# A hybrid decoder layer on one core: k projections evicted by ScalarE, queued sums between down products, and a new order of loads

## The chip, the cores and the metric

The kernel runs on 1 core of one Trainium2 chip. TensorE (PE) multiplies into PSUM; VectorE (DVE), ScalarE (ACT) and GpSimd (POOL) work beside it; SyncE (SP) issues nearly all DMAs. Each engine takes its instructions strictly in the order of its own queue. The metric is the device time of one launch in microseconds (us), the median of several runs.

## The reference

One decoder layer on a sequence of 1024 tokens of width 1024, in float32:

```python
hn = rmsnorm(x, attn_norm_w)
da_q, da_k, da_v, ml_qk, ml_v, ml_o, ml_i, ml_f = split_projection(hn @ w_in)
da_out = diff_attention(da_q, da_k, da_v, lam, slopes)      # 4 heads, causal, ALiBi
qk = silu(causal_dwconv(ml_qk, mlstm_conv_w, mlstm_conv_b)) # width 4
mq, mk = split(qk)                                          # mLSTM queries and keys
ml_out = sigmoid(ml_o) * rmsnorm(mlstm_chunkwise(mq, mk * d**-0.5, ml_v, i_pre, logf))
x = x + concat(da_out, ml_out) @ w_out
u = causal_dwconv(rmsnorm(x, ffn_norm_w) @ w_up, ffn_conv_w, ffn_conv_b)  # D_FF 2816
gate, up = split(u)
x = x + (silu(gate) * up) @ w_down
return rmsnorm(x, final_norm_w)
```

## The kernel before

**Products.** Every float32 operand is split into a high and a low part (`split`, lines 109 to 116: ACT writes the high part on line 112, DVE or POOL subtracts on line 113), and one product is three matmuls of 128x128 by 128x512 (`mm3`, lines 155 to 157; `mm3b`, lines 160 to 162). Split weights lie in eight `w` tiles in rotation; raw weights land in two `wf` tiles.

**Start.** The projections that feed the mLSTM's convolution come first, as columns: `ct` 0 to 3 are q, `ct` 4 to 7 are k, each in two halves `hf` of 512 tokens. q halves are copied out of PSUM by ACT (lines 350, 355) and scaled in SBUF with the row `RB` of inverse norms (line 363, 128x1024). For k the loop of lines 364 to 376 takes the banks `sa`/`sb`, `mm` and `big` in turn, and DVE takes each half out of PSUM and scales it in one instruction (line 369, 128x512). The same loop stores and begins POOL's sums of rows of `w_down` (`store_sums`, `down_sums`: lines 311 to 325; POOL on line 319, DMAs on lines 316 and 325), loads and splits `wo`, the weights of the o projection (line 375, four pieces), and runs the convolution of a q column (`conv_qk`: ACT line 339, three DVE instructions on line 341, ACT's Silu on line 342). The gate matmuls follow (line 384, first on bank `sb`, then on `sa`; DVE copies them out on line 385), the convolutions of the k columns, and the o projections (`o_unit`, on `wo`), two of which stand before the gates' transposes (line 429).

**Down projection.** It is a Strassen-like scheme of seven block products, in the order p = 1, 2, 7, 5, 6, 4, 3 (`PORDER`), each of 11 steps, 77 in all; a step is 12 matmuls, three for each of four row tiles `tt`. `steps` counts them through as k. `dprep_to(k + 1 + DLEAD)` prepares step k+4: the weight load for every second step (`wload`, line 1060), sums of activations for p = 2, 7, 6, 4 (line 1103), and two splits. `fill(k)` issues the larger loads at given steps: activations (`load`, line 1042) and the residual `x2` (lines 1081, 1090). Products alternate between two sets of banks; the last product takes up the `big` banks that p = 6 wrote. At a product's end `evac` adds its four PSUM banks into the outputs on DVE (line 1144): 4 adds after p = 1, 2, 4, 3, 8 after p = 5, 20 after p = 6; `half1` (ACT line 1164, DVE line 1172) follows p = 2 and 6, `finish` follows p = 4 and the last product.

**Order.** The order on each queue is not the order of the lines. A planner places instructions as it holds them to be ready; between instructions that are ready at once the earlier line goes first. The order is fixed when the kernel is built.

Of the kernel before, what the change touches and what calls it, by code (L numbers as in the profile page):

```python
# [13 lines left out]
AF = mybir.ActivationFunctionType  # L14
ALU = mybir.AluOpType
# [5 lines left out]
NT = S // P  # L21
# [18 lines left out]
def tile_hybrid(ctx: ExitStack, tc: tile.TileContext, I: dict, out: bass.AP):  # L40
    nc = tc.nc
    V = nc.vector
    A = nc.scalar
# [22 lines left out]
    def sm8(n=8, name="s8"):  # L66
        return sp.tile([P, n], F32, name=name, tag=name)
# [37 lines left out]
    x2d = dp.tile([NT, P, D], F32, name="x2d")  # L105
# [15 lines left out]
    HV = (slice(0, 512), slice(512, 1024))  # L121
# [21 lines left out]
    def getw(ahead):  # L143
        n = used[0]
        used[0] += 1
        while len(made) < min(n + 1 + ahead, len(specs)):
            made.append(wpiece(*specs[len(made)]))
        return made[n]
# [34 lines left out]
    def rotate(n):  # L183
        return (mmps, lambda: big([P, 512]), lambda: small([P, 512]))[n % 3]()
# [57 lines left out]
    def col_piece(ct):  # L242
        cw[ct, 0], cw[ct, 1] = wpiece(I["w_st"][ct], None, V)
# [38 lines left out]
    RB = pr0.t([P, S], tag="RB")  # L282
# [19 lines left out]
    M = [pq.t([P, S], tag="mqk", bufs=8) for _ in range(8)]  # L302
# [6 lines left out]
    pairs = list(range(NJ // 2))  # L309
# [12 lines left out]
    def store_sums(n=1):  # L322
        for i, g, u in (dsum.pop(0) for _ in range(min(n, len(dsum)))):
            for k, f in enumerate((g, u)):
                nc.sync.dma_start(wsum[i, k], f)
# [4 lines left out]
    def col_mm(ps, ct, kc, hf):  # L330
        k = slice(kc % 4 * P, (kc % 4 + 1) * P)
        w = cw[ct, kc // 4]
        mm3(ps, w[:, 0, k], w[:, 1, k], *xpart(kc, hf), kc == 0, kc == KC - 1)
# [30 lines left out]
    for ct in range(4, 8):  # L364
        for hf in range(2):
            ps = rotate(2 * ct + hf)
            for kc in range(KC):
                col_mm(ps, ct, kc, hf)
            V.tensor_tensor(M[ct][:, HV[hf]], ps, RB[:, HV[hf]], op=ALU.mult)
        store_sums()  # L370
        down_sums()
        if ct == 4:
            col_piece(7)
        elif ct == 6:
            wo = [getw(0) for _ in range(4)]
        conv_qk(ct - 4)
# [367 lines left out]
    x2 = []  # L744
# [323 lines left out]

    def fill(k):

        if k == 1:
            load(a21[:, 0:4, :], "A21", (0, 4))
        elif k == 3:
            load(a12, "A12", (4, NP - 1))
        elif k == 5:
            load(a21[:, 4:8, :], "A21", (4, 8))
        elif k == 7:
            load(a21[:, 8:, :], "A21", (8, NP))
        elif k in (6, 8, 9, 10):
            tt = (6, 8, 9, 10).index(k)  # L1080
            nc.sync.dma_start(x2[tt], x2d[tt])
        elif k == 11:
            load(a12[:, NP - 5:, :], "A12", (NP - 1, NP))
        elif k == 13:
            load(a22[:, 0:6, :], "A22", (0, 6))
        elif k == 17:
            load(a22[:, 6:, :], "A22", (6, NP))
        elif k in (20, 22, 24, 26):
            tt = 4 + (k - 20) // 2
            nc.sync.dma_start(x2[tt], x2d[tt])  # L1090
        elif k == 19:
            nc.sync.dma_start(fin, I["final_norm"].partition_broadcast(P))
            V.tensor_scalar(fin, fin, RSC, None, op0=ALU.mult)
# [40 lines left out]
    x2 = [pd.t([P, D], tag="x2", bufs=8) for _ in range(NT)]  # L1134
# [8 lines left out]
    def add(dst, x, y=None):  # L1143
        V.tensor_tensor(dst, dst if y is None else x, x if y is None else y, op=ALU.add)

    def evac(p, tt, ps):
        h0, h1 = HV
        c11, c12, c21, c22 = x2[tt][:, h0], x2[tt][:, h1], x2[tt + 4][:, h0], x2[tt + 4][:, h1]
        if p in (1, 7):
            A.activation(acc[p, tt], ps, AF.Copy)  # L1150
        if p == 6:
            a1, a7 = acc[1, tt], acc[7, tt]
            add(a1, ps)
            add(a7, a1)
            add(c22, a7)
            add(c21, a7)
            add(c12, a1)
        for dst in {1: [c11], 2: [c11], 5: [c12, c22], 4: [c21], 3: [c12]}.get(p, ()):
            add(dst, ps)

    def half(tt, h, part):

        j = pd.t([P, 512], tag="junk")
        A.activation(j, x2[tt][:, HV[h]], AF.Square, accum_out=part)
# [3 lines left out]
    def half1(tt, h):  # L1168

        half(tt, h, part1[:, tt:tt + 1])  # L1170
        xx = x2[tt][:, HV[h]]
        V.tensor_tensor(xx, xx, fin[:, HV[h]], op=ALU.mult)

    def finish(tts, h):

        n = len(tts)
        c = slice(tts[0], tts[0] + n)
        v = sm8(n, f"vx{n}")
        V.tensor_scalar(v, part1[:, c], 1.0 / D, EPS, op0=ALU.mult, op1=ALU.add)
        for tt in tts:  # L1180
            half(tt, h, part2[:, tt:tt + 1])
        V.scalar_tensor_tensor(v, part2[:, c], 1.0 / D, v, op0=ALU.mult, op1=ALU.add)
        if n == 1:
            r = newton(v)
        else:
            r = rsqrt(v, n, "x")
            V.tensor_scalar(r, r, 1.0 / RSC, None, op0=ALU.mult)
        a_, b_ = HV[1 - h], HV[h]
        for i, tt in enumerate(tts):
            xx, ri = x2[tt], r[:, i:i + 1]  # L1190
            A.activation(xx[:, a_], xx[:, a_], AF.Copy, scale=ri)
            V.scalar_tensor_tensor(xx[:, b_], xx[:, b_], ri, fin[:, b_], op0=ALU.mult, op1=ALU.mult)
            if tt == 3:
                A.dma_start(out[tt, :, a_], xx[:, a_])
                nc.sync.dma_start(out[tt, :, b_], xx[:, b_])
            else:
                nc.sync.dma_start(out[tt], xx)

    k = 0
    TAIL = 5  # L1200
    for n, p in enumerate(PORDER):
        ps = banks(n)
        last = n == len(PORDER) - 1
        for i in range(NP - TAIL if last else NP):
            dprep_to(k + 1 + DLEAD)
            fill(k)
            for tt in range(4):
                dmm(ps[tt], k, tt, i == 0, i == NP - 1)
            k += 1
        if not last:  # L1210
            for tt in range(4):
                evac(p, tt, ps[tt])
            if p == 2:
                for tt in range(4):
                    half1(tt, 0)
            elif p == 6:
                for tt in range(4, NT):
                    half1(tt, 1)
            elif p == 4:
                finish(range(4, NT), 0)  # L1220
        else:
            dprep_to(len(steps))
            for tts in LAST:
                for tt in tts:
                    for i in range(TAIL):
                        dmm(ps[tt], k + i, tt, False, i == TAIL - 1)
                    evac(p, tt, ps[tt])
                finish(tts, 1)
    psA.close()
    pd.close()  # L1230
# [64 lines left out]
```

## Time and profile before

| | us |
|---|---|
| median of 3 runs | 1242.09 (1241.46 to 1242.48) |
| profiled execution, its time | 1244.75 |
| profiled execution, its span | 1242.8 |
| PE busy | 1195.4 (96%) |
| DVE busy | 906.0 (73%) |
| ACT busy | 568.0 (46%) |
| POOL busy | 479.5 (39%) |
| DMA, mean over the span | 123 GB/s |

The profiled execution lies 2.66 us above the median and has 1.95 us outside its span. Times in rows are us from the start of the span. PE is busy nearly throughout, so the rows to look at are the few in which it waits, and what came last there.

### The profile page before, as it was taken

What the parts mean: (1) busy time and instruction counts of PE and PEld (TensorE: products, weight loads), DVE (VectorE), ACT (ScalarE), POOL (GpSimd) and SP (SyncE); (2) the same over time, 40 slices, a digit from 0 to 9 for tenths busy, and PEclk for the clock granted to TensorE, in tenths of its full rate; (3) what the DMA queues carried; (4) which work ended last, traced back from release to release, by engine and by line L of the source; (5) the groups of instructions that cost most, each with busy time, mean ns of one, the idle gap of its engine ahead of it and who ended that gap; (6) DMA issues with size and microseconds to landing.
All of it is one profiled execution on the core that took longest, in us unless ns stands there. A gap on an engine that the chain in (4) does not pass through costs nothing.

```text
span 1242.8 us, 15880 instructions
## 1 busy us (share of the span) xinstructions
PE 1195.4 (96%) x5600; PEld 973.8 (78%) x5600; DVE 906.0 (73%) x1568; ACT 568.0 (46%) x1106; POOL 479.5 (39%) x364
## 2 busy tenths in 40 slices
PE   7996999999999999999899999999999999999996
PEld 6884877888778878888688888888888887888775
DVE  5589232566667777679998878788787786986774
ACT  6533223333666665444543444434434344544443
POOL 0474410003443431001788888787787600000000
PEclk9997999999999999999999999999999999999999
DMA  8756442214212252333122222212212169623223
GB/s 310 234 215 243 163 170 78 76 68 156 74 51 52 68 167 97 119 111 111 46 91 102 85 99 71 85 68 85 100 71 85 51 212 380 244 96 98 73 94 135
DMA packets 60015, 153.26 MB, mean 123 GB/s; under 512 B 5984, under 2 KB 10272, under 8 KB 59936
## 3 DMA queue, kind: packets, MB, share of 16 engines
q1 hardware_dynamic: 59648, 151.47, 35.9%
q8 instruction: 44, 0.72, 0.2%
q10 hardware_dynamic: 288, 0.79, 0.2%
q14 instruction: 35, 0.29, 0.1%
HBM read 112.35 MB, written 35.68 MB: 119 GB/s over the span
## 4 chain that ended last, share of the span: by engine, by line
PE 80%; DVE 7%; DMA 4%; ACT 3%; POOL 2%; issue 2%; SPq 1%; ACTq 0%; POOLq 0%; DVEq 0%
PE mm L157 6%; PE mm L155 6%; PE mm L156 6%; PE mm L160 4%; PE mm L161 4%; PE mm L162 4%; PE big L157 4%; PE big L155 4%; PE big L156 4%; PE big L160 3%; PE big L161 3%; PE big L162 3%; PE sb L724 3%; POOL vda L319 2%; PE sa L157 2%; PE sa L155 2%
## 5 line engine op out<-in xcount | busy, mean ns | idle before, releaser
L112 ACT ACTIVATE w<-wf 128x512 fp32r<-128x512 f32 x162 | 99.0, 624 | 136.6 <-POOL w L113 25.4
L113 DVE TENSOR_TENSOR w<-wf,w 128x512 fp32r<-128x512 f32 x130 | 110.8, 861 | 38.1 <-ACT w L112 33.5
L981 DVE SCALAR_TENSOR_TENSOR y<-x2b,fcw,y 128x1022 f32<-128x1022 f32 x44 | 88.7, 2056 | 0.0
L980 DVE SCALAR_TENSOR_TENSOR y<-x2b,fcw,y 128x1023 f32<-128x1023 f32 x44 | 74.2, 1726 | 10.3 <-ACT y L979 10.3
L113 POOL TENSOR_TENSOR w<-s,w 128x512 fp32r<-128x512 f32 x40 | 69.3, 1733 | 6.5 <-ACT w L112 6.5
L113 POOL TENSOR_TENSOR w<-wu,w 128x512 fp32r<-128x512 f32 x40 | 67.5, 1687 | 2.1 <-ACT w L112 2.1
L113 POOL TENSOR_TENSOR w<-wf,w 128x512 fp32r<-128x512 f32 x32 | 45.3, 1418 | 59.5 <-ACT w L112 47.0
L319 POOL TENSOR_TENSOR vda<-vda 128x512 f32<-128x512 f32 x24 | 42.7, 1794 | 65.0 <-DMA vda<-in_w_down_dram 64.2
L155 PE MATMUL mm<-xb,w 128*128 128x512 f32 x168 | 66.8, 397 | 0.0
L156 PE MATMUL mm<-xb,w 128*128 128x512 f32 x168 | 66.4, 395 | 0.0
L157 PE MATMUL mm<-xb,w 128*128 128x512 f32 x168 | 66.4, 395 | 0.0
L699 DVE CUSTOM_DVE_ANT_0 s<-big,B 128x128 f32<-128x128 f32 (+7 forms) x64 | 47.6, 755 | 14.4 <-PE big L697 12.8
L979 ACT ACTIVATE y<-x2b,fcw 128x1024 f32<-128x1024 f32 x44 | 52.3, 1236 | 10.5 <-DVE x2b L970 9.1
L160 PE MATMUL big<-w 128*128 128x512 f32 x132 | 52.4, 398 | 3.8 <-ACT w L112 3.0
L915 POOL TENSOR_TENSOR s<-wu 128x512 f32<-128x512 f32 x22 | 38.4, 1745 | 43.9 <-DMA wu<-in_w_up_dram 43.9
L701 ACT ACTIVATE s<-s,mb 128x128 f32<-128x128 f32 (+7 forms) x64 | 49.3, 772 | 11.7 <-DVE mb L700 10.6
L161 PE MATMUL big<-w 128*128 128x512 f32 x132 | 51.9, 393 | 0.0
L162 PE MATMUL big<-w 128*128 128x512 f32 x132 | 51.5, 391 | 0.0
L112 ACT ACTIVATE w<-s 128x512 fp32r<-128x512 f32 x45 | 28.3, 629 | 50.5 <-PE mm L157 16.1
L916 POOL TENSOR_TENSOR s<-s,wf 128x512 f32<-128x512 f32 x22 | 42.5, 1933 | 20.0 <-DMA wf<-in_w_up_dram 18.2
L112 ACT ACTIVATE w<-hb 128x512 fp32r<-128x512 f32 x41 | 25.7, 628 | 51.8 <-PE big L162 24.2
L724 PEld LDWEIGHTS sb<-vda,aT 128*128 128x128 f32 x288 | 36.2, 190 | 15.3 <-ACT aT L721 14.5
(507 smaller groups left out, 3787.1 us busy)
## 6 DMA issues: line engine op xcount, KB each, us to landing
wf<-in_w_up_dram SPq DMA_DIRECT2D x22, 512.0 KB, 4.5
wu<-in_w_up_dram SPq DMA_DIRECT2D x22, 512.0 KB, 3.4
actd<-y SPq DMA_DIRECT2D x21, 512.0 KB, 2.6
wf<-in_w_st_dram SPq DMA_DIRECT2D x12, 512.0 KB, 4.0
vda<-in_w_down_dram SPq DMA_DIRECT2D x12, 512.0 KB, 6.4
wsum<-vda SPq DMA_DIRECT2D x12, 512.0 KB, 2.8
wf<-in_w_mv_dram SPq DMA_DIRECT2D x12, 512.0 KB, 4.6
wf<-wsum SPq DMA_DIRECT2D x12, 512.0 KB, 3.4
```

The costliest lines, as they stand in the source:

```text
L112: A.activation(dst[:, 0, :], src, AF.Copy)
L113: loeng.tensor_tensor(dst[:, 1, :], src, dst[:, 0, :].bitcast(F32), op=ALU.subtract)
L155: PE.matmul(ps, sh, mh, start=first, stop=False)
L156: PE.matmul(ps, sh, ml, start=False, stop=False)
L157: PE.matmul(ps, sl, mh, start=False, stop=last)
L160: PE.matmul(ps, sh, w[:, 0, :], start=first, stop=False)
L161: PE.matmul(ps, sl, w[:, 0, :], start=False, stop=False)
L162: PE.matmul(ps, sh, w[:, 1, :], start=False, stop=last)
L319: GP.tensor_tensor(dst, x_, y, op=ALU.subtract)
L724: PE.matmul(ops, aT[:, b * P:(b + 1) * P], vda[k // 2][:, k % 2, h * P:(h + 1) * P], start=k == 0, stop=k == qt)
L980: V.scalar_tensor_tensor(y[:, 1:], u[:, :S - 1], cw[:, 1:2], y[:, 1:], op0=ALU.mult, op1=ALU.add)
L981: V.scalar_tensor_tensor(y[:, 2:], u[:, :S - 2], cw[:, 0:1], y[:, 2:], op0=ALU.mult, op1=ALU.add)
```

## The change

Three parts. (1) In the loop over the k columns ACT copies each half out of PSUM, and one DVE instruction for each column then scales it in SBUF. (2) In the down projection the adds after a product, and the `half1` and `finish` that follow, go into a list `later`; each step of the next product issues three entries of it behind its preparation. In the last product the adds of a group of row tiles are issued together behind the group's matmuls. (3) In `fill` the activation loads move: A21's first part from step 1 to 2, A12's from 3 to 4, A21's second from 5 to 6, A21's third from 7 to 12, A12's last from 11 to 12; the four x2 loads go from steps 6, 8, 9, 10 to 8, 9, 10, 11.

```diff
@@ -366,7 +366,8 @@
             ps = rotate(2 * ct + hf)
             for kc in range(KC):
                 col_mm(ps, ct, kc, hf)
-            V.tensor_tensor(M[ct][:, HV[hf]], ps, RB[:, HV[hf]], op=ALU.mult)
+            A.activation(M[ct][:, HV[hf]], ps, AF.Copy)
+        V.tensor_tensor(M[ct], M[ct], RB, op=ALU.mult)
         store_sums()
         down_sums()
@@ -1068,18 +1069,16 @@
     def fill(k):
-        if k == 1:
+        if k == 2:
             load(a21[:, 0:4, :], "A21", (0, 4))
-        elif k == 3:
+        elif k == 4:
             load(a12, "A12", (4, NP - 1))
-        elif k == 5:
+        elif k == 6:
             load(a21[:, 4:8, :], "A21", (4, 8))
-        elif k == 7:
+        elif k in (8, 9, 10, 11):
+            nc.sync.dma_start(x2[k - 8], x2d[k - 8])
+        elif k == 12:
             load(a21[:, 8:, :], "A21", (8, NP))
-        elif k in (6, 8, 9, 10):
-            tt = (6, 8, 9, 10).index(k)
-            nc.sync.dma_start(x2[tt], x2d[tt])
-        elif k == 11:
             load(a12[:, NP - 5:, :], "A12", (NP - 1, NP))
@@ -1143,20 +1142,25 @@
+    later = []
+    def work(n):
+        for _ in range(min(n, len(later))):
+            later.pop(0)()
     def evac(p, tt, ps):
...
         if p == 6:
             a1, a7 = acc[1, tt], acc[7, tt]
-            add(a1, ps)
-            add(a7, a1)
-            add(c22, a7)
-            add(c21, a7)
-            add(c12, a1)
-        for dst in {1: [c11], 2: [c11], 5: [c12, c22], 4: [c21], 3: [c12]}.get(p, ()):
-            add(dst, ps)
+            pairs = [(a1, ps), (a7, a1), (c22, a7), (c21, a7), (c12, a1)]
+        else:
+            pairs = [(dst, ps) for dst in {1: [c11], 2: [c11], 5: [c12, c22], 4: [c21], 3: [c12]}.get(p, ())]
+        later.extend(lambda d=d, x=x: add(d, x) for d, x in pairs)
@@ -1204,6 +1208,7 @@
             dprep_to(k + 1 + DLEAD)
             fill(k)
+            work(3)
             for tt in range(4):
                 dmm(ps[tt], k, tt, i == 0, i == NP - 1)
@@ -1211,13 +1216,11 @@
             if p == 2:
-                for tt in range(4):
-                    half1(tt, 0)
+                later.extend(lambda tt=tt: half1(tt, 0) for tt in range(4))
             elif p == 6:
-                for tt in range(4, NT):
-                    half1(tt, 1)
+                later.extend(lambda tt=tt: half1(tt, 1) for tt in range(4, NT))
             elif p == 4:
-                finish(range(4, NT), 0)
+                later.append(lambda: finish(range(4, NT), 0))
@@ -1225,6 +1228,7 @@
                     for i in range(TAIL):
                         dmm(ps[tt], k + i, tt, False, i == TAIL - 1)
                     evac(p, tt, ps[tt])
+                work(len(later))
                 finish(tts, 1)
```

## Rows read from the trace of the kernel before

**Rows 1.** The waits of PE over the whole span, longest in total first: engine, bank and line that waited, what ended the wait, us in total, times, longest.

```profile
PE sa L384 <- DVE mqk L369: 10.1, 1, 10.1
...
PE big L160 <- ACT w L112: 3.0, 1, 3.0
PE mm L161 <- DVE w L113: 2.6, 1, 2.6
...
PE big L160 <- DVE x L1144: 0.8, 1, 0.8
```

**Rows 2.** The timeline of PE from 97 to 130 us: start, us, engine, line, operation and tiles, and in brackets the idle time before and what ended it.

```profile
97.74 3.87 PE L384 MATMUL sb<-xb,wg 128*16 128x512 f32 x16
111.74 6.45 PE L384 MATMUL sa<-xb,wg 128*16 128x512 f32 x16 [10.12 <-DVE mqk L369]
...
129.00 0.67 PE L429 MATMUL sb<-cst,gs 16*128 16x16 f32 x8
```

**Rows 3.** The timeline of DVE over the same stretch, its order being its queue's.

```profile
103.21 0.68 DVE L369 TENSOR_TENSOR mqk<-big,RB 128x512 f32<-128x512 f32 x1
...
105.28 5.80 DVE L341 SCALAR_TENSOR_TENSOR ta<-mqk,par,ta 128x1021 f32<-128x1021 f32 x3
111.00 0.68 DVE L369 TENSOR_TENSOR mqk<-sa,RB 128x512 f32<-128x512 f32 x1
111.60 1.27 DVE L341 SCALAR_TENSOR_TENSOR ta<-mqk,par,ta 128x1021 f32<-128x1021 f32 x1
...
115.78 1.55 DVE L113 TENSOR_TENSOR w<-wf,w 128x512 fp32r<-128x512 f32 x1
...
123.94 0.67 DVE L385 COPY gs<-sa 16x512 f32<-16x512 f32 x1
```

**Rows 4.** The timeline of ACT: an earlier copy out of PSUM (line 355), and its queue from 103 to 115 us.

```profile
53.19 0.60 ACT L355 ACTIVATE mqk<-sb 128x512 f32<-128x512 f32 x1 [3.91 <-PE sb L157]
...
103.98 1.24 ACT L339 ACTIVATE ta<-mqk,par 128x1024 f32<-128x1024 f32 x1 [2.23 <-DVE mqk L369]
107.65 1.06 ACT L342 ACTIVATE mqk<-ta 128x1024 f32<-128x1024 f32 x1 [2.43 <-DVE ta L341]
112.97 1.06 ACT L342 ACTIVATE mqk<-ta 128x1024 f32<-128x1024 f32 x1 [4.26 <-DVE ta L341]
113.93 1.13 ACT L112 ACTIVATE w<-wf 128x512 fp32r<-128x512 f32 x2
```

**Rows 5.** The instructions of lines 369 and 363: count, durations in ns (least, median, most), first and last start, shapes.

```profile
L369 DVE TENSOR_TENSOR mqk<-mm,RB x3: 675/677/682, 73.2 to 115.2; 128x512 f32<-128x512 f32 x3
...
L363 DVE TENSOR_TENSOR mqk<-mqk,RB x4: 1216/1768/2318, 55.2 to 59.7; 128x1024 f32<-128x1024 f32 x4
```

**Rows 6.** The timeline of PE where steps 5, 6 and 7 of the down projection begin.

```profile
1026.92 0.39 PE L160 MATMUL big<-w 128*128 128x512 f32 x1
...
1032.78 0.79 PE L160 MATMUL big<-w 128*128 128x512 f32 x1 [2.97 <-ACT w L112]
...
1036.96 0.40 PE L160 MATMUL big<-w 128*128 128x512 f32 x1
```

**Rows 7.** The timeline of ACT at the split of step 6's weights (tile `bw`).

```profile
1032.10 0.63 ACT L112 ACTIVATE w<-bw 128x512 fp32r<-128x512 f32 x1 [3.82 <-DMA bw<-in_w_down_dram]
```

**Rows 8.** The timeline of SP's queue at the beginning of the loads into the tiles of the down projection (line 1042: activations; line 1060: weights).

```profile
1024.78 0.37 SPq L1042 DMA_DIRECT2D a<-actd  x1
1025.24 0.46 SPq L1060 DMA_DIRECT2D bw<-in_w_down_dram  x1
1025.75 1.75 SPq L1042 DMA_DIRECT2D a<-actd  x2
```

**Rows 9.** DMA issues of four stretches, one row each: tiles, queue, count, KB each, median us from issue to landing. In order, those issued at 1024.78, 1025.24 and 1025.75 us, and those issued from 1009 to 1016 us.

```profile
a<-actd SPq DMA_DIRECT2D x1, 1024.0 KB, 5.9
...
bw<-in_w_down_dram SPq DMA_DIRECT2D x1, 512.0 KB, 6.8
...
a<-actd SPq DMA_DIRECT2D x1, 1536.0 KB, 10.4
...
wf<-in_w_down_dram SPq DMA_DIRECT2D x2, 512.0 KB, 5.6
```

**Rows 10.** The timeline of DVE at the end of product 6: the first of its 20 adds (line 1144), the four instructions of line 1172 behind the last, and the next split.

```profile
1166.89 1.28 DVE L1144 TENSOR_TENSOR acc<-acc,big 128x512 f32<-128x512 f32 x2
...
1178.92 2.48 DVE L1172 TENSOR_TENSOR x<-x,fin 128x512 f32<-128x512 f32 x4
1181.33 0.68 DVE L113 TENSOR_TENSOR w<-a,w 128x512 fp32r<-128x512 f32 x1
```

**Rows 11.** The timeline of PE at the same place: step 59 begins, waits, and step 60 begins.

```profile
1178.42 0.62 PE L160 MATMUL mm<-w,w 128*128 128x512 f32 x2
...
1182.06 0.97 PE L161 MATMUL mm<-w,w 128*128 128x512 f32 x2 [2.58 <-DVE w L113]
...
1185.39 0.59 PE L160 MATMUL mm<-w 128*128 128x512 f32 x1
```

**Rows 12.** Stretches: from and to, length, busy us (and instructions) of PE, its weight loads, DVE, ACT and POOL, then the granted clock of PE (1.00 is 2.4 GHz), the DMA share and GB/s.

```profile
110.00:120.00 10.00, 8.26 (x25) 3.92 (x26) 8.26 (x8) 3.34 (x4) 4.34 (x3) 0.63 0.87 290
...
1029.70:1042.40 12.70, 9.73 (x37) 7.84 (x37) 9.72 (x16) 4.38 (x8) 0.00 (x0) 0.87 1.05 394
...
1179.00:1186.00 7.00, 4.42 (x13) 3.17 (x12) 7.00 (x12) 1.62 (x5) 0.00 (x0) 0.76 0.13 32
```

## The prediction

> **What bounds the kernel now.** I read the page's busy shares first: PE is busy 96% of the span, so a change gains only where PE waits or runs at its lower clock. The second view is the waits of PE by line [rows 1]. Three waits belong to the parts of this change: 10.1 us at the gate matmuls (line 384) for DVE's eviction of a k half (line 369), 3.0 us for an ACT split and 2.6 us for a DVE split in the down projection. The third view is the timeline of each engine around these places, for what stands ahead of the late instruction on its queue. The reader is to see that in the first and third place DVE was not slow at the instruction that PE missed; it came to it late.
>
> A wait costs more than its length, because the clock falls with it: 0.63, 0.87 and 0.76 of 2.4 GHz in the stretches that hold the three waits [rows 12], so 1.2 GHz for part of each. So I count from where PE should have been. A down step is 2.72 us: from the beginning of step 7 (1036.96) to that of step 59 (1178.42) are 52 steps [rows 6, 11].
> - Gates: the second half was due at 97.74 + 3.87 = 101.61, began at 111.74 and took 6.45 instead of 3.87 [rows 2]. Lost: 10.1 + 2.6 = 12.7 us.
> - Step 6 was due at 1026.92 + 2.72 = 1029.64, step 7 at 1032.36; step 7 began at 1036.96 [rows 6]. Lost: 4.6 us.
> - Step 60 was due at 1178.42 + 2.72 = 1181.14 and began at 1185.39 [rows 11]. Lost: 4.25 us.
>
> **Part 1, k evictions by ACT.** It removes eight DVE instructions of 0.68 us and adds four of 128x1024, which in the same shape took 1.22 to 2.32 us [rows 5]: 5.4 us go, 4.9 to 9.3 come. DVE's work doesn't fall. ACT gets eight copies of 0.60 [rows 4], 4.8 us. What changes is who frees bank `sa`: no longer DVE, which reached the eviction at 111.00 although the bank's product had ended before 97.74.
>
> One would hope for all 12.7 us. I don't, because ACT's queue waits for DVE as well. In DVE's queue the eviction of the last column's first half stands between the second and the third convolution instruction of column 6 (the group at 105.28 is the last of column 5 and the first two of column 6; 111.60 is the third of column 6) [rows 3]. The planner held the bank to be full at that point. The copy becomes ready at the same point, but on ACT, and there it falls between the Silu of column 5 (107.65) and that of column 6 (112.97) [rows 4]. The former waits for DVE's convolution, so the copy can't pass it. How early can it start? Ahead of column 5's last convolution instruction DVE loses the two evictions of column 6, 0.6 us of queue each (one of them is the row at 103.21), and gains, ahead of it or behind it, the scaling of column 6, 1.22 to 2.32. The Silu then starts between 107.65 - 1.2 = 106.4 and 106.4 + 2.3 = 108.7 and takes 1.06; the first convolution instruction of column 6 on ACT (1.24, line 339) [rows 4] may stand between; the copy takes 0.60. PE goes on between 108.1 and 111.6, instead of 111.74; I take 109.8, the middle, for a gain of 2. The gates still run slowly, since PE has idled 8 us.
>
> What is late next: the last piece of `wo`, split by 117.3 (115.78 + 1.55) [rows 3]. The first o unit would start near 116.2 and needs it after 18 of its 24 matmuls (0.227 each, a twelfth of 2.72), at 120.3, so it is in time. Then the gates' transposes, at 129.0 now [rows 2], need DVE's copy of the gates, which ended at 124.6 [rows 3]; this caps the gain at 4.4 as long as DVE's queue ends there. Bounds of this part: 0 and 4.4; a loss is a rival below. Behind line 429 the gates' chain, the loads of the v weights and the chunks hang on PE or on each other, not on a clock of their own, so the gain is carried on.
>
> The rows of line 363 spread from 1216 to 2318 ns while POOL was summing, those of line 369 only from 675 to 682 [rows 5]. The Trainium skill (SBUF — State Buffer, Who interferes with whom) has a rule that speaks against this change: a DVE instruction with two SBUF inputs contends with a GpSimd instruction that reads SBUF, one with a single SBUF input doesn't. The trace agrees. By that rule each scaling may cost 2.32, DVE would be 3.9 us poorer, and the time would be that of the first rival.
>
> **Part 2, queued sums.** Behind product 6 DVE runs 20 adds and four instructions of line 1172 in one block from 1166.89 to 1181.33, 0.60 each, and only then the next split, for which step 59 waits [rows 10, 11]. In the changed source the preparation of step 59 stands ahead of the first three entries, and each later preparation ahead of the next three. A split that is ready then goes first. Per step of product 4 DVE has 3 x 0.6 + 2 x 0.6 = 3.0 us against PE's 2.72, so over the eight steps that empty the list (24 entries) it falls 2.3 us behind; the splits lead by three to four steps, 8 to 11 us, so PE doesn't see it. Gain: 4.25 at most; I take 4.0. Queued behind the adds are only the squares on ACT and the banks: the `big` banks of product 6 are free after 16 entries, six steps into product 4, and are wanted 11 steps after its start. After products 1, 2 and 5 PE waits for nothing now, so nothing is to be had there. In the last group PE waits 0.8 us for an add [rows 1]; that add still follows its matmuls, so I count 0.
>
> **Part 3, later loads.** The first load into the new tiles is A21's first part (1024 KB, issued 1024.78, landing after 5.9 us, at 1030.7); step 6's weights go behind it (1025.24, 6.8 us, at 1032.0); then 1536 KB of A12 (1025.75, 10.4 us, at 1036.2) [rows 8, 9]. They land one behind another, 512 KB in 1.35 us and 1536 KB in 4.1, so 0.37 MB per us. ACT's split follows at 1032.10 and PE at 1032.78 [rows 6, 7]. With A21 at step 2, `wload` of step 6 stands ahead of it and goes first, at 1024.78. It then lands as a 512 KB load does with less ahead of it, 5.6 us in the nearest row [rows 9], at 1030.4; taking off what the present first load shows (5.9 for 1024 KB, less 1.35 for the half) it is 4.5 us, at 1029.3. With 0.7 from landing to PE, step 6 starts at 1030.0 (by 5.6: 1031.1) against 1029.64 due. Gain: 4.6 - 0.4 = 4.2 at best, 1.7 if it lands after 5.6 and the slow stretch comes as before (1.45 of the 4.6); I take 4.0, since so short a wait (0.8 in rows 1) leaves the clock alone. Price on the other side: all later loads move back by 512 KB at most, 1.4 us, except A21's third part and the last of A12, which go behind the x2 loads, 2 MB or 5.5 us later. Step 11's weights come to about 1040.8 for a need at 1042; the third part of A21 to about 1051, wanted by sums of product 2 whose splits lead by four steps. Near, but covered.
>
> **Sum.** 2.0 + 4.0 + 4.0 = 10.0 us off a profiled span of 1242.8, so 1232.8 there; the runs' median lies 0.7 below that span, 1242.1, so **1232.1**. By the bounds (0 + 1.7 + 4.0 and 4.4 + 4.2 + 4.25) 1236.4 to 1229.2.
>
> **Rivals.**
> - *DVE stays the bound in the first stage.* Scalings at 2.32 us keep column 5's Silu and the copy where the eviction was: PE goes on at 111.6. For it: POOL is summing through most of this stretch. Against: two evictions fall away. Gain 8.0: 1234.1. Chance 0.21.
> - *The copy passes.* The planner puts it ahead of column 5's Silu, PE goes on at 101.6, and the next wait is for the last piece of `wo` or the gates' copies: 4.4 + 8.0, 1229.7; if DVE's queue is reordered as well so that these come early, the whole 12.7: 1221.4. Against: the Silu is ready about 2.5 us before that bank is full. Chance 0.12, a third of it for the far end.
> - *One of the down parts does not do what it says.* The planner still sets the adds in a block, since DVE looks idle to it, or A21 is still first at the door. One loss of 4.25 or 4.6 stays: 1236.2. Chance 0.09.
> - *Slower: ACT's queue takes DVE's place.* The copy falls behind column 6's Silu and the two splits of `wo` behind that. That Silu now has copy, scaling and line 339 ahead of its convolution: 112.97 plus 0.6 + 1.24 + 2 x 1.1 of collisions is 117.0; 1.06 of Silu, 1.13 of splits and 0.6 of copy give 119.8. From 119.7 on (111.74 + 8.0) this eats all that the down projection gains; with the three convolution instructions colliding too, 3 x 1.0, it is 122.8, 3.1 over: 1245.2. Against: the bank is full some 3 us before column 6's last convolution instruction. Chance 0.07.
> - The rest, 0.08, is a time near the present one: several of these bounds at once, each a little short.
>
> **How the numbers follow.** Forecast 1232.1, chance 0.43; its own range 1229 to 1236. Below 1226 lies only the far end of the second rival (0.04); above 1239 lie the slower rival and the rest (0.15). So 1226 to 1239, with 0.81 inside. A measurement of this kernel can tell about 0.2%, 2.5 us, from no change: faster (under 1239.6) 0.43 + 0.21 + 0.12 + 0.09 = 0.85, the same 0.08, slower (over 1244.6) 0.07.
>
> **What would show it.** In the profile after: line 369 as four SBUF instructions of 1.2 to 2.3 us; the wait of the gates on bank `sa` now ended by ACT, starting at 101.6 and ending between 108 and 111.6, right behind a Silu. Step 6 begins within a microsecond of step 5's end and its weights are the first load of the down tiles. Behind product 6 DVE alternates splits and threes of adds, and step 59 takes 2.72. Wrong would be: gates that go on at 101.6, or after 112; a new PE wait for line 1103 or for an x2 load around 1040 to 1055; a wait for a split in product 4.

## The result and the profile after

The changed kernel takes 1231.89 us, the median of 5 runs (1231.05 to 1236.98), beside 1242.48 for the kernel before (5 runs, 1241.46 to 1244.14): 10.6 us less. The ratio over the runs is 0.9907, 95% interval 0.988 to 0.9934; that of the two medians is 0.9915. Its profiled execution took 1232.53 with a span of 1230.7, 12.1 below the span before. Lines behind line 369 stand one further on (385 for 384, 430 for 429, 1043 for 1042, 1061 for 1060), behind `fill` one less (1143 for 1144), and behind `evac` four more (1176 for 1172). One thing has to be known to read the traces: between 650 and 990 us, where the granted clock is 1.00, matmuls follow each other at 230.2 ns in nine of the fourteen traces, 229.5 in three and 233.3 in two (4.6 us over that stretch). Each kernel has one trace, so it is not shown whether the kernel or the execution sets this; I compare stretches and not only spans.

PE's waits over the whole span, as in [rows 1]:

```profile
PE sa L385 <- ACT mqk L369: 6.6, 1, 6.6
...
PE sa L160 <- ACT w L112: 1.8, 1, 1.8
...
PE big L160 <- DVE x L1143: 0.8, 1, 0.8
...
PE sb L430 <- DVE gs L386: 0.3, 1, 0.3
```

Both waits of the down projection are gone; that of the gates went from 10.1 to 6.6 and ends with ACT. A new one stands at the v projections: 1.8 us for a split of their weights. PE's timeline beside [rows 2]:

```profile
97.64 3.87 PE L385 MATMUL sb<-xb,wg 128*16 128x512 f32 x16
108.14 5.14 PE L385 MATMUL sa<-xb,wg 128*16 128x512 f32 x16 [6.63 <-ACT mqk L369]
...
124.14 0.41 PE L430 MATMUL sb<-cst,gs 16*128 16x16 f32 x4
124.84 0.42 PE L430 MATMUL sb<-cst,gs 16*128 16x16 f32 x4 [0.29 <-DVE gs L386]
...
166.56 0.50 PE L160 MATMUL sa<-w,xb 128*128 128x512 f32 x1 [1.81 <-ACT w L112]
```

The gates go on 3.6 us earlier and run 1.3 shorter, so the transposes come 4.9 earlier; the two later waits, of 0.3 and 1.8, cost 0.4 and 2.0 of that again. Two stretches tell the rest, the first of after, the second of before (columns as in [rows 12]):

```profile
168.00:174.00 6.00, 6.00 (x21) 4.78 (x21) 0.89 (x3) 0.92 (x2) 3.48 (x3) 0.72 0.56 196
```

```profile
313.00:321.00 8.00, 7.23 (x27) 5.72 (x28) 4.94 (x21) 3.29 (x11) 4.05 (x6) 0.79 0.43 116
```

Behind the wait of 1.8 us PE's granted clock is 0.72 from 168 to 174 us, which costs another 1.6, so only 0.9 us of the lead is left. From 313 to 321 us it is the kernel before that runs slowly, behind a wait of 1.9 us for a split (line 696); after waits 1.5 there and stays at 1.00, and by 321 us its lead is 2.95. The down projection begins at 1010.50 instead of 1013.27. ACT's timeline beside [rows 4]; in brackets the idle time before:

```profile
102.65 0.63 ACT L112 ACTIVATE w<-wf 128x512 fp32r<-128x512 f32 x1 [7.25 <-DMA wf<-in_w_mv_dram]
103.19 1.04 ACT L342 ACTIVATE mqk<-ta 128x1024 f32<-128x1024 f32 x1
104.13 0.58 ACT L369 ACTIVATE mqk<-big 128x512 f32<-128x512 f32 x1
104.61 0.62 ACT L112 ACTIVATE w<-wf 128x512 fp32r<-128x512 f32 x1
105.29 1.06 ACT L342 ACTIVATE mqk<-ta 128x1024 f32<-128x1024 f32 x1
106.37 1.24 ACT L339 ACTIVATE ta<-mqk,par 128x1024 f32<-128x1024 f32 x1
107.52 0.58 ACT L369 ACTIVATE mqk<-sa 128x512 f32<-128x512 f32 x1
113.85 1.06 ACT L342 ACTIVATE mqk<-ta 128x1024 f32<-128x1024 f32 x1 [5.76 <-DVE ta L341]
114.82 1.14 ACT L112 ACTIVATE w<-wf 128x512 fp32r<-128x512 f32 x2
```

The copy out of `sa` (107.52) stands behind column 5's Silu (105.29) and line 339, as forecast. New to me is the head of the list: ACT stands idle 7.25 us for the third raw piece of `wo`, and all below it is queued behind the split of that piece. DVE's timeline, of this stretch (beside [rows 3]) and behind product 6 (beside [rows 10]):

```profile
91.23 2.31 DVE L370 TENSOR_TENSOR mqk<-mqk,RB 128x1024 f32<-128x1024 f32 x1
93.47 3.59 DVE L113 TENSOR_TENSOR w<-wf,w 128x512 fp32r<-128x512 f32 x4
96.98 4.85 DVE L341 SCALAR_TENSOR_TENSOR ta<-mqk,par,ta 128x1022 f32<-128x1022 f32 x4
103.31 0.69 DVE L113 TENSOR_TENSOR w<-wf,w 128x512 fp32r<-128x512 f32 x1 [1.48 <-ACT w L112]
103.92 1.27 DVE L341 SCALAR_TENSOR_TENSOR ta<-mqk,par,ta 128x1021 f32<-128x1021 f32 x1
...
107.94 5.82 DVE L341 SCALAR_TENSOR_TENSOR ta<-mqk,par,ta 128x1023 f32<-128x1023 f32 x3
...
124.12 0.67 DVE L386 COPY gs<-sa 16x512 f32<-16x512 f32 x1
...
1160.70 0.69 DVE L1143 TENSOR_TENSOR acc<-acc,acc 128x512 f32<-128x512 f32 x1
1161.30 0.69 DVE L113 TENSOR_TENSOR w<-a,w 128x512 fp32r<-128x512 f32 x1
1161.90 0.69 DVE L113 TENSOR_TENSOR w<-wf,w 128x512 fp32r<-128x512 f32 x1
1162.50 1.29 DVE L1143 TENSOR_TENSOR x<-x,acc 128x512 f32<-128x512 f32 x2
1163.73 0.69 DVE L113 TENSOR_TENSOR w<-a,w 128x512 fp32r<-128x512 f32 x1
```

DVE idles too for that piece (103.31). Behind product 6 it now changes between adds and splits. SP's timeline, stretch of the `wo` loads and start of the down projection (beside [rows 8]):

```profile
94.73 0.80 SPq L325 DMA_DIRECT2D wsum<-vda  x2
95.58 0.78 SPq L316 DMA_DIRECT2D vda<-in_w_down_dram  x1
96.46 1.64 SPq L126 DMA_DIRECT2D wf<-in_w_mv_dram  x2
...
1012.61 0.42 SPq L1061 DMA_DIRECT2D bw<-in_w_down_dram  x1
1022.00 0.92 SPq L1043 DMA_DIRECT2D a<-actd  x2
```

Step 6's weights (1012.61) leave 9.4 us ahead of A21's first load; before, both left together at 1024.78 and 1025.24. The windows that hold steps 6 to 10 and 58 to 60 show PE busy throughout at a granted clock of 1.00 (columns as in [rows 12]):

```profile
1026.80:1040.00 13.20, 13.20 (x59) 10.91 (x59) 9.67 (x16) 5.20 (x10) 0.00 (x0) 1.00 1.05 396
1168.00:1176.00 8.00, 8.00 (x37) 6.61 (x36) 8.00 (x15) 4.69 (x10) 0.00 (x0) 1.00 0.19 72
```

From start to start the lead over before is 2.78 us at the first down step, 7.39 at step 11, 11.65 at step 60, 11.87 at step 61 and 12.04 at the last row tile: 2.78 for part 1, 4.61 for part 3, 4.48 for part 2 and 0.17 in the last group. The last 0.2 between steps 60 and 61 are the rest of step 59's wait: before, the first matmul of step 60 still took 0.42 us and not 0.23.

### The profile page after: what moved, and what is told of

Its sections match the earlier page's. It is cut to its first block, busy times and chain, and to the rows that moved or that the text cites. A ratio compares the mean times of both kernels' runs of the same rounds, so it can differ in the third digit from the quotient of the medians.

```text
span 1230.7 us, 15875 instructions
## 1 busy us (share of the span) xinstructions
PE 1191.1 (97%) x5600; PEld 972.0 (79%) x5600; DVE 907.1 (74%) x1564; ACT 572.1 (46%) x1114; POOL 479.7 (39%) x364
## 4 chain that ended last, share of the span: by engine, by line
PE 81%; DVE 9%; DMA 4%; ACT 3%; issue 2%; POOL 0%; SPq 0%; DVEq 0%; ACTq 0%; POOLq 0%
PE mm L157 6%; PE mm L155 6%; PE mm L156 6%; PE mm L160 4%; PE big L157 4%; PE big L155 4%; PE mm L161 4%; PE big L156 4%; PE mm L162 4%; PE big L160 4%; PE big L162 4%; PE big L161 4%; PE sb L725 3%; DVE ta L341 2%; PE sa L157 2%; PE sa L155 2%
## 5 line engine op out<-in xcount | busy, mean ns | idle before, releaser
L113 DVE TENSOR_TENSOR w<-wf,w 128x512 fp32r<-128x512 f32 x130 | 108.3, 844 | 35.7 <-ACT w L112 31.2
L319 POOL TENSOR_TENSOR vda<-vda 128x512 f32<-128x512 f32 x24 | 47.4, 1991 | 62.9 <-DMA vda<-in_w_down_dram 62.2
L725 PE MATMUL sb<-vda,aT 128*128 128x128 f32 x288 | 44.2, 289 | 3.7 <-ACT aT L722 3.1
```

The source lines that it names most:

```text
L113: loeng.tensor_tensor(dst[:, 1, :], src, dst[:, 0, :].bitcast(F32), op=ALU.subtract)
L725: PE.matmul(ops, aT[:, b * P:(b + 1) * P], vda[k // 2][:, k % 2, h * P:(h + 1) * P], start=k == 0, stop=k == qt)
```

## The experiments

My theory: (A) the copy of `sa` waits in ACT's queue for what DVE and the splits of `wo` do, so bank `sa` is not itself the price; A21's first load alone cost the 4.6 us; the interleaving of adds, not the list, saves the loss at step 59. The rival for each: the bank, the other moved loads, any queue. The tables' columns are read off PE's timeline. G is the start of the first gate half; "go on" the start of the second, "transposes" that of line 429 or 430, "down" that of the first down matmul, all less G; "length" runs from there to the last down matmul; "pace" is the mean distance of matmul starts from 650 to 990 us, in ns. "Down" holds the pace too: 229.5 takes 1.0 us off it, 233.3 adds 4.6. Ratios are to the kernel before on the same chip.

| kernel | go on | transposes | down | length | pace |
|---|---|---|---|---|---|
| before | 14.00 | 31.26 | 915.53 | 219.61 | 230.2 |
| after | 10.50 | 26.50 | 912.86 | 210.33 | 230.2 |
| part 1 alone | 11.01 | 27.01 | 910.66 | 217.96 | 229.5 |
| part 2 alone | 14.75 | 32.00 | 920.39 | 213.37 | 233.3 |
| one load at step 2 | 14.54 | 30.55 | 914.48 | 214.97 | 230.2 |
| that load by POOL | 13.88 | 30.00 | 914.02 | 218.64 | 230.2 |
| without part 1 | 14.09 | 30.22 | 919.78 | 210.32 | 233.3 |
| all sums at once | 11.22 | 28.61 | 912.37 | 211.69 | 230.2 |
| gates on `big` | 3.71 | 28.42 | 910.19 | 210.30 | 229.5 |
| late sums | 10.34 | 27.73 | 911.12 | 210.34 | 230.2 |
| both of these | 3.70 | 28.58 | 914.53 | 210.34 | 230.2 |
| pair left out | 11.56 | 28.72 | 911.47 | 210.31 | 230.2 |
| pair left out, `big` | 3.71 | 25.18 | 907.12 | 210.30 | 229.5 |
| pair later | 9.80 | 26.36 | 909.09 | 210.31 | 230.2 |

| kernel | median (range), runs | ratio, 95% interval |
|---|---|---|
| part 1 alone | 1239.36 (1237.45 to 1245.48), 10 | 0.9954, 0.9929 to 0.9978 |
| part 2 alone | 1238.84 (1236.38 to 1244.06), 10 | 0.9953, 0.993 to 0.9976 |
| one load at step 2 | 1239.0 (1235.37 to 1244.32), 10 | 0.9944, 0.9919 to 0.997 |
| that load by POOL | 1242.77, 1 | none |
| without part 1 | 1236.58 (1233.56 to 1241.01), 7 | 0.9936, 0.9908 to 0.9964 |
| all sums at once | 1234.66 (1233.25 to 1237.13), 4 | 0.992, 0.9896 to 0.9943 |
| gates on `big` | 1232.11 (1231.17 to 1239.6), 4 | 0.991, 0.9875 to 0.9945 |
| late sums | 1231.73 (1231.26 to 1232.83), 4 | 0.9895, 0.9875 to 0.9916 |
| both of these | 1235.09 (1229.65 to 1236.55), 6 | 0.9926, 0.9906 to 0.9947 |
| pair left out | 1230.37 (1230.07 to 1232.41), 4 | 0.9895, 0.9874 to 0.9917 |
| pair left out, `big` | 1229.52 (1226.52 to 1231.92), 4 | 0.9888, 0.9867 to 0.991 |
| pair later | 1229.54 (1226.7 to 1230.74), 4 | 0.9886, 0.9866 to 0.9906 |

The intervals are some 6 us wide, too wide to share out 10.6 us: the single parts' medians add up to more than the whole. The stretches decide.

**Part 1 alone.** The kernel before with the ACT copies and the scaling.

> Only the first part of the change (ScalarE copies the k halves out of PSUM, one scaling per column in SBUF). Theory A, ScalarE's queue and then DVE's queue bound the stage: the second gate half goes on at 108 to 109 us, the gates' transposes follow DVE's gate copies at about 124.8 (129.0 before), and of these 4.4 us some 2.8 are left where the down projection begins; 2.8 us off the time, near 1239.7. Rival, the first stage gives nothing by itself: gates go on at 111 to 112, time as before, within 0.5 us. Rival, all the lost time comes back: 10 to 12 us.

The gates go on 11.01 after G behind ACT, the transposes come 4.3 earlier than before, and both down waits stay. Of the lead 3.8 us are left at the down projection (4.9, less 1.0 for the pace), more than the 2.8 expected. The step-6 wait costs less here; see "part 2 alone".

**Part 2 alone.** The kernel after with the loads and the k evictions of before.

> Only the second part (adds queued, three per step). Theory A, the block of 24 DVE instructions behind product 6 was the whole cause of step 59's wait: step 59 takes 2.72 us, 4.25 off there and 0.4 in the last group of row tiles, 4.6 in all, near 1237.9; step 6 still loses 4.6. Rival, the earlier arrival of other work after the loads' change is what filled the hole: step 59 still waits, gain under 1 us.

No wait at step 59. The length is 6.24 shorter than before, 4.64 for the adds and the last group, as the next experiment shows, and 1.60 because the step-6 wait, still there, is 0.3 shorter (2.70) and did not slow the clock: the window that holds it is at 1.00.

```profile
1034.00:1046.00 12.00, 9.30 (x41) 7.37 (x40) 8.68 (x15) 4.28 (x8) 0.00 (x0) 1.00 1.05 394
```

So that wait costs 3.04 (213.37 - 210.33) or, where the clock falls as in the profile before, 4.64.

**One load at step 2.** The kernel before, with one line of part 3:

```diff
-        if k == 1:
+        if k == 2:
             load(a21[:, 0:4, :], "A21", (0, 4))
```

> The smallest piece of the third part: A21's first load at step 2 instead of 1, all other loads as before, so that on SP's queue only this load and the one of step 6's weights change places. Theory Q, the weights were held by SP's queue behind a load that waits for its tile: they are issued some 10 us earlier (near 1015), step 6 does not wait, 4.6 us off, near 1237.9, and the other moves of loads are worth nothing. Theory F (as predicted), both loads find the tiles free at the same moment (near 1024.8) and only land in another order: the weights are issued at 1024.8, PE waits 0.3 to 1.4 us, 1.7 to 4.2 off.

```profile
1016.14 0.42 SPq L1060 DMA_DIRECT2D bw<-in_w_down_dram  x1
1025.53 2.28 SPq L1042 DMA_DIRECT2D a<-actd  x3
```

These two rows of SP's timeline have changed places, and the step-6 wait is gone. The length falls by 4.64; what is left to 210.33 is again 4.64, which is part 2. The other moved loads add nothing to it.

**That load by POOL.** Here the step stays and the queue changes, so that SP is not held by this load:

```diff
...
-            load(a21[:, 0:4, :], "A21", (0, 4))
+            load(a21[:, 0:4, :], "A21", (0, 4), eng=GP)
```

> The kernel before with one edit: A21's first load is issued from GpSimd's queue, still at step 1; everything else stays on SP in its old order. Theory Q: SP is no longer held by that load, the weights of step 6 go out near 1015 us and step 6 does not wait: 4.6 us off. Theory F: the weights still can't be issued before their tile is free near 1024.8, and A21 competes with them as before: step 6 waits 2 to 3 us, 0 to 1 us off.

Step 6's weights leave at 1014.56 and step 6 does not wait. POOL issues A21's load only at 1028.75, and with 10.0 us from issue to landing it comes too late for DVE. DVE's and then PE's timeline:

```profile
1038.73 4.30 DVE L1103 TENSOR_TENSOR hb<-hb,a 128x512 f32<-128x512 f32 x7 [8.38 <-DMA a<-actd]
1042.95 0.68 DVE L113 TENSOR_TENSOR w<-bw,w 128x512 fp32r<-128x512 f32 x1
```

```profile
1043.69 0.68 PE L162 MATMUL big<-w 128*128 128x512 f32 x1 [3.40 <-DVE w L113]
```

Seven sums of product 2 wait for that load, the split for step 10 waits behind them, and PE waits 3.40 there. The clock falls with it (0.86 from 1038 to 1050 us), step 10 loses 5.3, and the length gains 1.0 on before instead of the 4.6 expected. The weights' delay is shown to come from SP's queue, but the load's place has a price on the other side as well.

**All sums at once.** The kernel after with `work(len(later))` for `work(3)`.

> The changed kernel, but the first step of the next product issues the whole list, not three entries. If three per step is what matters (theory A): behind product 6 the block of 24 DVE instructions, 14.4 us, is back, only one step's splits later: a step near 59 or 60 waits 1 to 3 us and runs slowly, 2 to 4.5 us lost against the changed kernel. Rival, it is enough that the next preparation stands ahead of the adds and DVE's lead covers the rest: nothing lost, within 0.5 us.

DVE's timeline has the block back, here 1162.93 to 1175.57, and PE misses a split (PE's row under it):

```profile
1173.16 2.49 DVE L1176 TENSOR_TENSOR x<-x,fin 128x512 f32<-128x512 f32 x4
1175.57 0.68 DVE L113 TENSOR_TENSOR w<-a,w 128x512 fp32r<-128x512 f32 x1
```

```profile
1176.31 0.74 PE L161 MATMUL mm<-w 128*128 128x512 f32 x2 [1.06 <-DVE w L113]
```

By the lengths the price is 1.36 us (211.69 - 210.33), under the 2 to 4.5 of my theory and over the 0.5 of the rival: the next step's preparation already stands ahead of the block. So of the 4.64 of part 2 about 3.3 come from issuing the adds behind a preparation, and 1.4 from three at a time.

**Without part 1.** The kernel after with DVE's evictions of before.

> The changed kernel without its first part (parts two and three alone). Theory A, the parts add up: 9.3 us off the kernel before (4.6 for step 6, 4.3 for step 59, 0.4 in the last group), near 1233.2 and 2.8 over the changed kernel; the gates wait for DVE at 111.7 as before. Rival, the first part is worth nothing net: the time of the changed kernel within 0.5 us.

The gates go on where they did before, the transposes come 1.0 earlier, since the late gate half took 5.28 and not 6.45, and the length is that of after. By these stretches part 1 and the other two do not touch each other.

**Gates on `big`.** The kernel after with the second gate half on a free bank:

```diff
-        gp = small([16, 512])
+        if hf:
+            flip[0] ^= 1
+        gp = big([16, 512]) if hf else small([16, 512])
```

> The changed kernel with the second half of the gates on a free bank of the big set instead of sa; the order of ScalarE's and DVE's queues is the same. So the wait for ScalarE's copy (6.6 us) is gone. Theory A, DVE's queue is the next bound: PE runs the gates at full clock from 101.5 to 105.4, then waits in the first o projection for the last piece of wo (split near 116.7), and the gates' transposes still wait for DVE's gate copy near 124.1 to 124.8: gain 0, within 0.5 us. Rival, the bank was the bound: transposes 6 to 8 us earlier, 5 to 8 us off.

PE's timeline, then ACT's:

```profile
103.47 3.87 PE L387 MATMUL big<-xb,wg 128*16 128x512 f32 x16
...
118.38 0.80 PE L160 MATMUL mm<-w,xb 128*128 128x512 f32 x1 [6.90 <-ACT w L112]
```

```profile
116.75 1.06 ACT L342 ACTIVATE mqk<-ta 128x1024 f32<-128x1024 f32 x1 [5.77 <-DVE ta L341]
117.71 1.14 ACT L112 ACTIVATE w<-wf 128x512 fp32r<-128x512 f32 x2
```

The whole 6.6 us wait is taken away and comes back as 6.9 in the first o unit, for `wo`'s last piece, which ACT splits behind column 6's Silu. In this kernel the bank is not the price.

**Late sums.** The kernel after with the first v unit's sums moved to the second unit, to let the v weights land earlier:

```diff
+        if tt == 1:
+            late_sums()
         if tt == 0:
-            late_sums()
...
```

> The changed kernel with one call of the late sums (a store and two loads of 512 KB on SP's queue) moved from the first v unit to the second. Theory A: the new wait of PE for the split of the v weights (1.8 us, where 1.6 us of the first stage's gain go) comes from the load of these weights queued and running beside the sums' traffic; it shrinks to under 0.5 and 1 to 1.6 us come off. Rival: the weights' load is late because of ScalarE's earlier splits, whatever else is on the queue; the wait stays at 1.5 to 1.8, gain 0.

The new wait at the v units is 1.0 instead of 1.8, between the two expectations. **Both of these** joins the last two edits:

> The kernel after, with the second half of the gate matmuls on a bank of big instead of sa, and the first v unit's sums begun one unit later. Theory A (the first stage is set by the chain of wo's third and fourth piece, not by bank sa): PE runs the gates through and then waits some 6.5 to 7 us in the first o unit for ACT's split of wo's last piece; the transposes of the gates start where they do with the sums moved alone, and the time is that kernel's, 1231.7 within 0.7. Rival B (bank sa is a price of its own): the 6.5 us wait goes and does not come back in full, 1229 or less.

The o unit's wait is 6.9 again. But the v wait is 1.7 with the same edit, so the sums of that unit are not what makes it; what sets it stays open. The time missed its expectation upwards. In the trace the down projection begins 3.4 later than with the late sums alone; 2.0 of that arise in the first v units, where the granted clock is 0.86 from 165 to 177 us, and 1.00 from 165 to 175 with the late sums.

**Pair left out.** The kernel with the late sums, in which the sixth pair of rows of `w_down` is neither loaded nor summed; the fifth pair's tiles are stored in its place, and the queue orders of ACT and DVE stay:

```diff
...
-        down_sums()
+        down_sums() if ct < 7 else dsum.append((pairs.pop(0), *last))
```

> The kernel after, with the first v unit's sums begun one unit later, and without the sixth pair of sums of rows of w_down: its two loads and POOL's four subtractions are left out, and the fifth pair's tiles are stored in its place, so the stores stay (that pair's sums are wrong). Queue orders of ACT and DVE are unchanged. Theory A (the copy that frees bank sa comes late because the queues of ACT and DVE stand waiting for wo's third piece, whose load goes behind that pair's load on SP's queue; and DVE's convolution of column 6 takes 5.8 us instead of 3.7 beside POOL's sums of that pair): wo's third load is issued 0.4 to 0.7 earlier and lands with 1 MB less around it, ACT's split of it starts 0.7 to 1.2 us earlier against the start of the gates, the gates go on 1.0 to 1.5 us earlier, column 6's convolution takes 3.7 us, the gates' transposes come 2 to 2.5 us earlier, time 1229.3. Rival B (the copies and splits are ACT's and DVE's own work that fills the stretch): nothing moves by more than 0.5, 1231.7.

Half of theory A held. Column 6's convolution takes 3.92 us instead of 5.82 without POOL beside it. But the load of `wo` leaves 0.65 us later against G than with the late sums, not earlier. On SP's queue three stores (1.63 us) stand ahead of it in place of two and a load (1.58), and the stores wait for POOL's earlier sums, which end 0.63 later. The gates go on 1.2 later. **With `big`** as well:

> The same without the sixth pair's loads and subtractions (that pair's sums are wrong), and with the second half of the gates on a bank of big. Theory A: the gates run through at full clock, PE waits for ACT's split of wo's last piece only about 2.5 us (it comes 3 us earlier than with the pair), then some 2 us for DVE's copy of the gates; the transposes come 3 to 5 us earlier than with the sums moved alone, time 1227 to 1228.5. Rival B: the 6.9 us wait for wo's last piece stays, 1231.7.

The o unit waits 5.04 instead of 6.9, not 2.5, for the same late piece. The transposes come 2.5 earlier than with the late sums, at 122.58, and then wait 0.46 for DVE's copy of the gates. Against the kernel with the pair left out, where ACT begins the split of the third piece at the same distance from G (6.07 us, 6.10 here), the bank alone brings the transposes 3.5 earlier (25.18 for 28.72): with the pair gone, the bank has a price.

**Pair later.** The same computation as after, with the pair moved to the seventh v unit and the late sums as above:

```diff
-        down_sums()
+        if ct < 7: down_sums()
...
+        if tt in (1, 6):
+            late_sums()
         if tt == 0:
-            late_sums()
...
```

> The same edit without leaving work out: the sixth pair of sums is moved from the k loop to a second late call, at the seventh v unit, beside the one at the second. SP's order changes with it: the loads of the second half of the v weights now stand behind three loads and two stores of sums. Theory A: in the first stage as without the pair (gates' transposes 2 to 2.5 us earlier), and then the v units wait 2 to 5 us for ACT's split of their weights, so the gain is given back: 1231 to 1234. Rival B: first stage unchanged, 1233 to 1236.

ACT's timeline, then DVE's:

```profile
102.75 0.63 ACT L112 ACTIVATE w<-wf 128x512 fp32r<-128x512 f32 x1 [4.73 <-DMA wf<-in_w_mv_dram]
...
107.62 0.57 ACT L369 ACTIVATE mqk<-sa 128x512 f32<-128x512 f32 x1
...
111.76 1.06 ACT L342 ACTIVATE mqk<-ta 128x1024 f32<-128x1024 f32 x1 [3.56 <-DVE ta L341]
```

```profile
107.74 3.92 DVE L341 SCALAR_TENSOR_TENSOR ta<-mqk,par,ta 128x1023 f32<-128x1023 f32 x3 [0.71 <-ACT ta L339]
```

No sums' load stands ahead of `wo`'s here. The gates go on 0.7 earlier than after, the v wait is 1.0 and not 2 to 5, and the down projection begins 3.8 earlier against G. At 1229.54 us it has the lowest median of the kernels that leave nothing out. Its interval overlaps that of after, so that it beats the change is likely and not shown.

One number joins all these traces. In the six that have ACT's copies and the gates on `sa`, the gates go on 5.49 or 5.50 us after ACT begins the split of `wo`'s third piece: 108.14 - 102.65 in after, 109.61 - 104.12, 108.41 - 102.91, 109.80 - 104.31, 110.50 - 105.01 and 108.25 - 102.75. In all six ACT works without a pause from that split to the copy. The chain from that load to PE is fixed; only the load's landing moves.

## Why the prediction was right, step by step

The time, 1231.89 for 1232.1, and the signs of all three parts were right, and no rival came. Three of the reasons were not.

**Part 1: size right, one link missed, one claim wrong.** That the copy sits behind column 5's Silu and PE goes on between 108.1 and 111.6 held, at the early end: 108.14. I built that range from DVE's and ACT's own work. What sets it is the landing of `wo`'s third piece. The change even delays its load, to 96.46 from 93.91. Before, the load left as soon as DVE's second split gave the raw buffer back (93.88). Now that split ends at 95.85, behind a scaling of 2.31 us (91.23), and the load leaves 0.6 later still. SP's waits after, from 88 to 101 us, show what else stood ahead:

```profile
SPq L325 <- POOL vda L319: 7.2, 1, 7.2
```

SP's stores wait until 94.73 for POOL's last subtraction (before until 92.75), and a load of `w_down` (95.58) follows them. POOL's last three subtractions ahead of these stores take 1.3 us each in all five traces without part 1; with it the first two of them take 2.2 in all nine and the last 1.7 to 2.3. That it is DVE's work beside them that slows them is argued, not shown. This is the fault of part 3 in another place, for 0.6 us: a ready load behind a store that waits. With the load out sooner the Silu could have come earlier still; I have not tried that alone.

"The gates still run slowly" was half right: 5.14 us here, 6.57 in other traces of the same copies, 5.2 to 6.45 with the waits of 10 us and more. And "the gain is carried on" is the step that failed: of the 4.9 us at the transposes 0.4 went into the wait for DVE's copy, 2.0 into the wait for the v weights and 1.6 into the low clock behind it, and 0.9 was left. Another 2.1 came between 285 and 321 us, in work that the prediction does not look at. That is not the luck of one profile: between the same two matmuls this stretch takes 33.8 to 34.3 us in the nine traces with part 1 and 35.2 to 35.9 in the five without. Why is not traced. So 2.78 against 2.0 is a balance of losses and gains that the prediction did not have, and that it lies so near is luck.

**The collisions.** Three of the four scalings took 1.2 us, one 2.31; the prediction's bounds were the right ones:

```profile
L370 DVE TENSOR_TENSOR mqk<-mqk,RB x4: 1207/1218/2314, 74.3 to 116.7; 128x1024 f32<-128x1024 f32 x4
```

Column 6's three convolution instructions took 5.82 beside POOL's sums and 3.92 without them. The rule of the Trainium skill that was weighed there (SBUF — State Buffer, Who interferes with whom) agrees with both. The first rival did not come: it asked for collisions at all the scalings, and only at one of four (91.23) was POOL already summing.

**Part 2: right, a little over its cap.** 4.48 against 4.0, capped at 4.25: the cap left out the slow first matmul of step 60. DVE falls behind PE as worked out and PE does not see it. The 0.17 of the last group was counted at nothing. It goes with the queued sums: the four traces without them lose it at the same two matmuls (1222.34 and 1222.60 in before), the ten with them do not.

**Part 3: size right, mechanism wrong.** I took it that the two loads leave together and land one behind another, so that changing their order would save one landing. In fact the weights were ready to leave 10 us earlier and stood on SP's in-order queue behind a load that was waiting for data. A view that I had not read says so, SP's waits before, from 1000 to 1040 us:

```profile
SPq L1042 <- DMA actd<-y: 14.2, 2, 9.4
```

A21's load (line 1042) reads what the last store of `y` has yet to write, and stood 9.4 us for it. Both experiments on that load show it. So the whole 4.61 was gained, outside the bounds 1.7 to 4.2, and the sums on landing orders had no part in it. A look at the waits of the issuing queue would have pointed to it at once.

**The sum.** The terms of the profile come to 12.04 where 10.0 was forecast, the medians to 10.6. So the time agrees better than its terms, and that is luck. Of the difference 1.6 may be the fallen clock at step 6 in the one profile of before, since two of the three traces that have that wait lack the fall. That is argued, not shown.

## What to carry to other kernels

When a transfer is late, first ask when it could have been issued: on an engine's in-order DMA queue one load that waits for its data holds all that are written behind it, and one line's order was worth 4.6 us here. Stores that wait do the same: behind those of POOL's sums `wo`'s load left 0.6 late. Before a bank's wait is credited to an edit, take the bank away: if the wait returns one instruction later, as 6.6 us did as 6.9, the bound is elsewhere, for that kernel: with POOL's pair left out the same bank was worth 3.5 us. And look for the one event with a fixed distance to the wait's end over several traces; here the 5.5 us from a split named the load behind it.

## What the runs showed of the hardware

Over the stretch from 650 to 990 us, at a granted clock of 1.00, matmuls of one shape started every 229.5, 230.2 or 233.3 ns, the same over the stretch within a trace and different between traces; whether the kernel or the execution makes the difference is not shown. In the down projection it was 226.7 in all fourteen. A wait of PE has no fixed price. At step 59 the same wait of 2.58 us cost 4.48 in before, at 0.76 from 1179 to 1186 us, and 2.87 with the load by POOL, at 1.00 from 1176 to 1186. At step 6 a wait of 2.70 cost 3.04 with the clock granted in full, and one of 2.97 cost 4.64 with 0.87 over the stretch. The gate half that takes 3.87 at full clock took 5.14 to 6.57 in the eleven traces where PE had idled 5.9 to 10.9 us before it, and the longer wait did not go with the longer half. Whether a DVE scaling of 128x1024 in SBUF meets POOL is decided at its start: of the 92 scalings in the fourteen traces (lines 363 and 370) each took 2.30 to 2.33 us where POOL was in a subtraction when it began, and 1.21 to 1.23 where it was not, even if one began 0.1 us later; such a subtraction took 2.2 to 2.3 us instead of 1.3.
